# An opening loop that ends in another order, and modulation blocks moved from the heads to the branch projections

## The chip, the cores and the metric

The kernel runs on one core of a Trainium2 chip, as one launch. The metric is the device time of one execution in microseconds (us). The engines are TensorE (PE, matrix products), VectorE (DVE), ScalarE (ACT), GpSimd (POOL) and SyncE (SP, which here only issues DMAs). Each engine takes its instructions strictly in the order in which they stand; between engines semaphores order the work.

## The reference

Two layers of an encoder trunk on x of 256 tokens by 1024 channels, in f32. Each layer has two sub-layers, both modulated by a vector c:

```
mod = silu(c) @ ada_w[l] + ada_b[l]              # 6 x 1024: sh1, sc1, g1, sh2, sc2, g2
h = rmsnorm(x, norm_mix_w) * (1 + sc1) + sh1
x = x + g1 * mixer(h)
h = rmsnorm(x, norm_ffn_w) * (1 + sc2) + sh2
x = x + g2 * ((gelu(a) * val) @ w_down)          # a, val: halves of causal_conv3(h @ w_up)
```

The mixer projects h to 4784 columns. Columns c_q and c_kv go through an RMS norm and a second projection (w_uq, w_ukv) to the queries, keys and values of an attention with 8 heads; k_rope gets the rotary sine and cosine. The columns q_m and k_m go through a causal convolution of width 4 and a silu to the queries and keys of an mLSTM with 8 heads, whose gates i and f are 16 more columns. Both results are projected (w_br_mla, w_br_mlstm), merged by two sigmoid gates, and projected by w_out.

## The kernel before, in words

**Products.** Channels lie on the 128 partitions, tokens along the free axis. A weight tile of 128x1024 is loaded by SP (`raw`), rounded by ScalarE to a high part (`whi`, a CAST of about 1 us), and VectorE takes the rest (`wlo = raw - whi`). A product is three matmuls: whi with the high part of h (`hh`), whi with the low part (`hl`), wlo with `hh`. They follow each other on TensorE at about 0.117 us each for 256 tokens. A *unit* is 256 columns of w_in: 48 matmuls, two weight tiles. `W.take` (line 161) hands out a unit's weights, and the tiles of the next unit are split in the slots of this one (`emit_piece`).

**Evictions.** Each unit has a generator (`conv_silu`, `c_evict`, `misc_evict`, `gate_evict`, ...) that reads its PSUM bank. `unit` (line 265) runs slots of 12 matmuls; at the start of each slot `advance` takes every living generator one `yield` further. A scheduler in the framework then orders the instructions of an engine, but no further apart than a window (`act.window`, `dve.window`, line 172 on): window 0 keeps the written order.

**Opening** (lines 1222 to 1320). The six units in `FIRST` (line 68) of layer 0 are computed together, block k of 128 channels by block, while the modulation of that block is computed from its weights. The first `NATIVE` = 2 units of the list multiply in plain f32 (`ua` with `raw`), the other four in three matmuls. Units 0, 1 hold c_q and part of c_kv, unit 2 the rest of c_kv and the *misc* block (gates i, f and k_rope), unit 3 the first quarter of q_m, units 9 and 10 the output gate. At k = 7 `rotary_finish` (line 445) makes the sine and cosine, and a dummy tangent makes ScalarE load the table for tangent and exponential.

**Mixer of layer 0** (line 605). The evictions of the opening's units start (lines 963 on): c_evict (squares for the norm, and a copy `cqkv` scaled by the norm's weight), misc_evict, then conv_silu of unit 3. Units 4, 5, 6 follow, each with its convolution (6 `z` instructions on VectorE per unit, then a tangent and `qm`/`km`). Beside them run `c_norms` (statistics by matmuls with `shares`, a power on GpSimd, a broadcast by matmul, then `ua`, `ub` as the high and low part of the normed c) and `gates` (a transpose to `gs`, a chain of some 20 small instructions to `LF`, matmuls for sums over time to `CS`, a transpose to `ats`, a scan `M`, which is spread over partitions through DRAM to `tgl`). `DELAYS` and `LATER` say by how many slots each step is held back. Then come w_uq and w_ukv, ten *filler* units (v_m, output gate, merge gates) among which the 8 + 8 heads run, the branch projections (line 1090 on), w_out, and the feed-forward part.

**Heads.** An attention head makes scores (`bank<-kall,qall`), VectorE the maxima (`sm`), ScalarE the exponentials, VectorE the RECIPROCAL of the sum, ScalarE `w<-w,sm`, TensorE transposes (`bank<-cst,w`).

**Modulation blocks.** All other columns of mod are made by `pump` (line 344), one block of 128 outputs at a time: SP loads 128x1024 weights (`ada`, 512 KB, two buffers), and one VectorE instruction multiplies and sums. 24 blocks per layer have to be done by the end of the branch projections: in layer 0 and 1 they are pumped from the fillers (`fill`, line 1051), two per filler, three in the fillers of `FILLERS_3`.

Almost all instructions bear the line of the helper that records them (L184, or L186 for its other branch), so rows are told apart by tile names.

Of the kernel before, what the change touches and what calls it, by code (L numbers as in the profile page):

```python
# [60 lines left out]
FILLERS_3 = (4, 5, 6, 7)  # L61
# [6 lines left out]
FIRST = (0, 1, 2, 9, 10, 3)  # L68
NATIVE = 2
DELAYS = dict(kr=6, c=1, gates=3)  # L70
MLA_DELAY = (3, 2)
MASK_SLOTS = (4, 3) + (2,) * 6
LATER = (2, 2, 2, 1)
# [119 lines left out]
def hybrid_trunk(ctx, tc, a):  # L193
# [82 lines left out]
    def fm_steps(out, w, h, ks, msl, h0=0, start=True, stop=True):  # L276

        wh, wl = w
        hh, hl = h
        for i, k in enumerate(ks):  # L280
            first = start and i == 0
            last = stop and i == len(ks) - 1
            pe.matmul(out, wh.at(k, msl), hh[:, h0 + k, :], start=first, stop=False)
            pe.matmul(out, wh.at(k, msl), hl[:, h0 + k, :], start=False, stop=False)
            pe.matmul(out, wl.at(k, msl), hh[:, h0 + k, :], start=False, stop=last)
# [13 lines left out]
    def pair_slots(w, h, outs=None, split=False):  # L299


        if outs:
            def slot(ks):
                def run():
                    for k in ks:
                        for j in range(2):
                            fm_steps(outs[j], w, h, [k], slice(j * P, (j + 1) * P),
                                     start=k == 0, stop=k == KB - 1)
                return run

            return [slot(range(2 * i, 2 * i + 2)) for i in range(4)], outs
        if split:
            outs = [bank()[:, :T], bank()[:, :T]]
        else:
            b = bank()
            outs = [b[:, :T], b[:, T:2 * T]]

        def slot(j, k0):
            def run():
                fm_steps(outs[j], w, h, range(k0, k0 + 4), slice(j * P, (j + 1) * P),  # L320
                         start=k0 == 0, stop=k0 == 4)
            return run

        return [slot(j, k0) for j in range(2) for k0 in (0, 4)], outs
# [120 lines left out]
    def rotary_finish():  # L445
# [8 lines left out]
        act.activation(trigq[64:128], trig[64:128], AF.Copy, scale=qscale)  # L454
# [150 lines left out]
    def mixer(l, n, begun):  # L605
# [35 lines left out]
        def c_evict(i0, srcs):  # L641
            sqs = []
            for i, src in enumerate(srcs):
                sq = w256()
                act.activation(sq, src, AF.Square)
                b = i0 + i
                act.activation(cc_[:, b, :], src, AF.Copy, scale=ppc(l, "qn", b) if b < 3 else ppc(l, "kvn", b - 3))
                sqs.append(sq)
            yield
# [7 lines left out]
        def misc_evict(misc):  # L657
            act.activation(gt, misc[0:40], AF.Identity, bias=ppc(l, "gb", 0, 0, 40))
            r1 = w256()
            r2 = w256()  # L660
            dve.tensor_tensor(r1[64:96], misc[64:96], trig[64:96], ALU.mult)
            dve.tensor_tensor(r2[64:96], misc[96:128], trig[96:128], ALU.mult)
            kr = w256(tag="kr", bufs=1)
# [297 lines left out]


        if begun:
            h, first = begun
            for i in range(2):
                spawn(c_evict(2 * i, first[i][:2]))
            spawn(c_evict(4, first[2][:1]))
            spawn(misc_evict(first[2][1]))
            advance()
# [12 lines left out]
        for i in range(4):  # L982
            if 3 + i in first:
                spawn(conv_silu(2 * i, first[3 + i][:2]))
            else:
                slots, outs = pair_slots(W.take(), h)
# [64 lines left out]
        def fill():  # L1051
            i = left.pop(0)
            run_filler(i, ada=(0, 1, 2) if i in FILLERS_3 else (0, 2))
# [35 lines left out]

        ya = [(yah[:, 2 * i:2 * i + 2, :], yal[:, 2 * i:2 * i + 2, :]) for i in range(2)]  # L1090
        for c in range(2):
            for y, merge in ((ya, merge_a), (yl, merge_b)):
                w = W.take()
                for q in range(2):
# [10 lines left out]
                    unit([slot(0), slot(1)], merge(4 * c + 2 * q, b))  # L1105
# [145 lines left out]
    act.activation(warm, warm, AF.Sin)  # L1251
# [25 lines left out]
    for k in range(KB):  # L1277
# [23 lines left out]
        if k == KB - 1:  # L1301
            rotary_finish()
            act.activation(warm, warm, AF.Tanh)
# [14 lines left out]
    W.queue_split(W.at)  # L1318
    W.flush()
    pe.window, act.window, dve.window, gp.window = 1000, 8, 8, 2  # L1320
# [151 lines left out]
```

## Time and profile before

| what | value |
|---|---|
| three runs | 830.99, 831.08, 834.4 us; median 831.08 |
| the profiled execution | 829.05 us, of which the span from first to last instruction is 827.3 us |
| TensorE busy | 794.7 us of the span, 6452 matmuls |
| VectorE busy | 688.4 us |
| ScalarE busy | 502.0 us |
| mean granted TensorE clock | 0.986 of 2.4 GHz |
| DMA | 188.34 MB, 228 GB/s over the span |

Busy time counts an engine's instructions, and TensorE's are pipelined, so that short waits hide in it; a stretch is read by when its matmuls start and by what the engines beside it wait for. The clock that TensorE is granted is either full (2.4 GHz, shown as 1.00) or half (0.50). A wait is named with the engine that ended it.

### The profile page before, as it was taken

The numbers are of one execution on the slowest core, as the hardware profiler recorded it, in microseconds if no ns is written. First come the engines' busy times: TensorE is split into PE (matmuls) and PEld (weight loads), VectorE is DVE, ScalarE is ACT, GpSimd is POOL, SyncE is SP. The second block draws the span as 40 slices with busy tenths as digits, with TensorE's granted clock in tenths as the row PEclk, the third lists the DMA queues.
The fourth block names the chain that finished last, engine by engine and source line by source line (L and its number), as shares of the span: only waits on it lengthen the run. The fifth ranks groups of instructions, "written<-read, shape, count | busy, mean of one in ns | idle before, by whom it ended". The sixth has DMA issues, their size and how long they took to land.

```text
span 827.3 us, 16719 instructions
## 1 busy us (share of the span) xinstructions
PE 794.7 (96%) x6452; PEld 777.5 (94%) x6452; DVE 688.4 (83%) x1241; ACT 502.0 (61%) x918; POOL 79.0 (10%) x98
## 2 busy tenths in 40 slices
PE   5998989999999999999999999899999999999995
PEld 4998888999999999999999999799999999999995
DVE  5957988888989998888968987898887998888752
ACT  5674747664558766653548674676455876665551
POOL 4700020100010000000111001110011000000010
PEclk9998999999999999999999999999999999999998
DMA  9984587787765775468985468878754566546841
GB/s 338 396 287 133 184 328 259 237 284 258 239 219 175 244 239 182 142 199 305 327 328 179 133 203 303 278 250 284 255 180 159 178 204 197 182 142 202 296 125 51
DMA packets 57072, 188.34 MB, mean 228 GB/s; under 512 B 6576, under 2 KB 8352, under 8 KB 56992
## 3 DMA queue, kind: packets, MB, share of 16 engines
q1 hardware_dynamic: 55520, 183.89, 66.4%
q10 hardware_dynamic: 864, 2.23, 0.8%
q0 software_dynamic: 608, 1.16, 0.6%
q8 instruction: 50, 0.82, 0.4%
q14 instruction: 30, 0.25, 0.1%
HBM read 185.07 MB, written 1.06 MB: 225 GB/s over the span
## 4 chain that ended last, share of the span: by engine, by line
PE 57%; DVE 8%; DMA 4%; issue 3%; ACT 1%; DVEq 0%; POOLq 0%; POOL 0%; ACTq 0%
PE bank L184 57%; DMA ada<-in_ada 4%; DVE wlo L184 3%; DVE ada L184 2%; DVE w L184 1%; DVE hl L184 1%; DVE ub L184 0%; DVE z L184 0%; ACT whi L184 0%; DVE x L184 0%; ACT w L184 0%; DVE ua L184 0%; ACT ua L184 0%; ACT rs L184 0%; ACT sq L184 0%
## 5 line engine op out<-in xcount | busy, mean ns | idle before, releaser
L184 DVE TENSOR_TENSOR wlo<-raw,whi 128x1024 fp32r<-128x1024 f32 (+3 forms) x276 | 305.4, 1113 | 30.0 <-PE bank L184 10.5
L184 ACT CAST whi<-raw 128x1024 fp32r<-128x1024 f32 (+3 forms) x276 | 261.1, 955 | 114.1 <-PE bank L184 78.6
L184 PE MATMUL bank<-hh,whi 128*128 128x256 f32 x974 | 278.8, 287 | 0.0
L184 PE MATMUL bank<-hh,wlo 128*128 128x256 f32 x975 | 273.9, 281 | 1.1 <-DVE wlo L184 1.1
L184 PE MATMUL bank<-hl,whi 128*128 128x256 f32 x975 | 274.3, 282 | 0.0
L184 PEld LDWEIGHTS bank<-hh,wlo 128*128 128x128 f32 x975 | 184.3, 189 | 1.5 <-DVE wlo L184 1.5
L184 PEld LDWEIGHTS bank<-hl,whi 128*128 128x128 f32 x975 | 184.6, 189 | 0.9 <-DVE hl L184 0.3
L184 PEld LDWEIGHTS bank<-hh,whi 128*128 128x128 f32 x974 | 184.3, 189 | 1.1 <-issue 0.2
L184 DVE SCALAR_TENSOR_TENSOR ada<-ada,sact 128x1024 f32<-128x1024 f32 x96 | 118.4, 1237 | 21.0 <-DMA ada<-in_ada 20.7
L184 DVE SCALAR_TENSOR_TENSOR z<-bank,pp,z 128x255 f32<-128x255 f32 (+2 forms) x208 | 95.2, 477 | 17.0 <-ACT z L184 14.7
L184 PE MATMUL bank<-gh,wlo 128*128 128x256 f32 x352 | 99.0, 281 | 1.1 <-DVE wlo L184 1.1
L184 PE MATMUL bank<-gl,whi 128*128 128x256 f32 x352 | 99.1, 281 | 0.0
L184 PE MATMUL bank<-gh,whi 128*128 128x256 f32 x352 | 98.9, 281 | 0.0
L184 PEld LDWEIGHTS bank<-gh,wlo 128*128 128x128 f32 x352 | 66.3, 188 | 1.3 <-DVE wlo L184 1.3
L184 PEld LDWEIGHTS bank<-gl,whi 128*128 128x128 f32 x352 | 66.3, 188 | 0.0
L184 PEld LDWEIGHTS bank<-gh,whi 128*128 128x128 f32 x352 | 66.3, 188 | 0.0
L184 PE MATMUL bank<-ub,whi 128*128 128x256 f32 (+1 forms) x256 | 59.2, 282 | 0.0
L184 ACT ACTIVATE z<-bank,pp 128x256 f32<-128x256 f32 x96 | 49.1, 558 | 9.6 <-PE bank L186 5.6
L184 ACT ACTIVATE w<-z 128x256 f32<-128x256 f32 x60 | 25.0, 416 | 38.8 <-DVE z L184 37.1
L186 PE MATMUL bank<-hh,whi 128*128 128x256 f32 x146 | 46.1, 316 | 0.0
L184 PEld LDWEIGHTS bank<-ub,whi 128*128 128x128 f32 x256 | 43.9, 189 | 0.0
L186 PE MATMUL bank<-hh,wlo 128*128 128x256 f32 x145 | 42.7, 294 | 0.0
(253 smaller groups left out, 1390.3 us busy)
## 6 DMA issues: line engine op xcount, KB each, us to landing
ada<-in_ada SPq DMA_DIRECT2D x96, 512.0 KB, 5.1
raw<-in_w_up SPq DMA_DIRECT2D x88, 512.0 KB, 4.5
raw<-in_w_in SPq DMA_DIRECT2D x64, 512.0 KB, 5.6
raw<-in_w_down SPq DMA_DIRECT2D x32, 384.0 KB, 4.4
raw<-in_w_down SPq DMA_DIRECT2D x32, 320.0 KB, 3.9
raw<-in_w_out SPq DMA_DIRECT2D x16, 512.0 KB, 5.2
raw<-in_w_first SPq DMA_DIRECT2D x8, 512.0 KB, 8.1
raw<-in_w_bra SPq DMA_DIRECT2D x8, 512.0 KB, 5.2
```

The lines of the kernel that those rows point to most:

```text
L184: r = f(*args, **kw)
L186: r = f(*args, **kw)
```

## The change

Six things are written differently. (1) `FIRST` becomes 3, 2, 0, 1, 9, 10, so that unit 3 (a convolution's) and unit 2 (with the misc block) are the native ones and end first in each k. (2) The dummy activation ahead of the opening is a Silu and not a Sin, the dummy Tanh behind it is gone, and a dummy Exp comes later, in `widen`; `trigq` is moved behind the evictions. (3) ScalarE and VectorE stay in written order (window 0) from the opening until `widen` has been advanced twice: the convolution's first two steps, the gates' copy, the weight split, the rest of misc_evict, then c_evict. (4) c_evict takes the squares of its blocks first; in layer 0 the copies `cqkv` are made by VectorE. (5) The unit after the opening runs its matmuls with wlo behind those with whi (`late_lo`); the delays of the norm's sums, c_norms and gates change. (6) `FILLERS_3` is gone: every filler pumps two blocks, and every second of the eight half units of the branch projections pumps one, in both layers.

```diff
-FILLERS_3 = (4, 5, 6, 7)
+BRANCH_PUMPS = (0, 2, 4, 6)
-FIRST = (0, 1, 2, 9, 10, 3)
+FIRST = (3, 2, 0, 1, 9, 10)
-DELAYS = dict(kr=6, c=1, gates=3)
+DELAYS = dict(kr=6, shares=2, c=3, gates=1)
-LATER = (2, 2, 2, 1)
+LATER = (2, 2, 2, 0)
...
-            pe.matmul(out, wl.at(k, msl), hh[:, h0 + k, :], start=False, stop=last)
+            if not late_lo:
+                pe.matmul(out, wl.at(k, msl), hh[:, h0 + k, :], start=False, stop=last)
+        for i, k in enumerate(ks):
+            if late_lo:
+                pe.matmul(out, wl.at(k, msl), hh[:, h0 + k, :], start=False, stop=stop and i == len(ks) - 1)
...
-        act.activation(trigq[64:128], trig[64:128], AF.Copy, scale=qscale)
...
+                sqs.append(sq)
+            for i, src in enumerate(srcs):
                 b = i0 + i
-                act.activation(cc_[:, b, :], src, AF.Copy, scale=ppc(l, "qn", b) if b < 3 else ppc(l, "kvn", b - 3))
-                sqs.append(sq)
-            yield
+                gain = ppc(l, "qn", b) if b < 3 else ppc(l, "kvn", b - 3)
+                if begun:
+                    dve.tensor_scalar(cc_[:, b, :], src, gain, None, ALU.mult)
+                else:
+                    act.activation(cc_[:, b, :], src, AF.Copy, scale=gain)
+            for _ in range(1 + (DELAYS["shares"] if begun else 0)):
+                yield
...
+        def widen():
+
+            yield
+            yield
+            act.window = dve.window = 8
+            act.activation(warm, warm, AF.Exp)
...
-            for i in range(2):
-                spawn(c_evict(2 * i, first[i][:2]))
-            spawn(c_evict(4, first[2][:1]))
-            spawn(misc_evict(first[2][1]))
-            advance()
+            conv, misc = conv_silu(0, first[3][:2]), misc_evict(first[2][1])
+            cs = [c_evict(i0, src) for i0, src in ((4, first[2][:1]), (0, first[0][:2]), (2, first[1][:2]))]
+            W.queue_split(W.at)
+            next(conv)
+            next(conv)
+            next(misc)
+            W.flush()
+            next(misc)
+            for c in cs:
+                next(c)
+            act.activation(trigq[64:128], trig[64:128], AF.Copy, scale=qscale)
+            sides.extend([conv, misc] + cs[1:] + cs[:1] + [widen()])
...
-            run_filler(i, ada=(0, 1, 2) if i in FILLERS_3 else (0, 2))
+            run_filler(i, ada=(0, 2))
...
-                    unit([slot(0), slot(1)], merge(4 * c + 2 * q, b))
+                    unit([slot(0), slot(1)], merge(4 * c + 2 * q, b), ada=(0,) if half in BRANCH_PUMPS else ())
+                    half += 1
...
-    act.activation(warm, warm, AF.Sin)
+    act.activation(warm, warm, AF.Silu)
...
-            act.activation(warm, warm, AF.Tanh)
...
-    W.queue_split(W.at)
-    W.flush()
-    pe.window, act.window, dve.window, gp.window = 1000, 8, 8, 2
+    pe.window, gp.window = 1000, 2
```

Three places show what this does to the order.

The first is ScalarE at the end of the opening, from the second half of the rotary table on; `bank_211` is the first unit of `FIRST`, `bank_212` the second, `bank_213` to `bank_216` the four others, `whi_639` and `whi_680` the first weight tile of unit 4. Before:

```order
L184 ACTIVATE trig<-w_89_599 32x256
L184 ACTIVATE w_119_679<-bank_211 128x256
L184 ACTIVATE trigq<-trig 64x256
L184 ACT_TABLE_LOAD
L184 ACTIVATE warm<-warm 128x1
L184 CAST whi_639<-raw_635 128x1024
L184 CAST whi_643<-raw_637 128x1024
L184 ACTIVATE cqkv_676<-bank_211,pp 128x256
L184 ACTIVATE w_120_682<-bank_211 128x256
```

And now:

```order
L184 ACTIVATE trig<-w_89_599 32x256
L184 ACTIVATE z_669<-bank_211,pp 128x256
L184 ACTIVATE z_671<-bank_211,pp 128x256
L184 ACTIVATE gt_659<-bank_212,pp 40x256
L184 CAST whi_680<-raw_665 128x1024
L184 CAST whi_684<-raw_667 128x1024
L184 ACTIVATE w_123_692<-bank_212 128x256
L184 ACTIVATE w_124_695<-bank_213 128x256
L184 ACTIVATE w_125_697<-bank_213 128x256
L184 ACTIVATE w_126_701<-bank_214 128x256
L184 ACTIVATE w_127_703<-bank_214 128x256
L184 ACTIVATE trigq<-trig 64x256
```

The convolution's start (`z`), the gates' copy and the weight split (`whi`) now stand ahead of the squares (`w_123` on); the table load and the dummy behind it, which stood ahead of the split, stand six rows further down than what is shown, and the scaled copies `cqkv` are gone from ScalarE.

On VectorE at the same place, from the end of the rotary arguments (`w_89`), before; `z_721` is the convolution of unit 3, `gs` the transposed gates:

```order
L184 TENSOR_SCALAR w_89_599<-kr_105,csts 32x256
L184 TENSOR_TENSOR wlo_640<-raw_635,whi_639 128x1024
L184 TENSOR_TENSOR wlo_644<-raw_637,whi_643 128x1024
L184 TENSOR_TENSOR w_124_695<-bank_213,trig 32x256
L184 TENSOR_TENSOR w_125_696<-bank_213,trig 32x256
L184 TENSOR_TENSOR kr_699<-w_124_695,w_125_696 32x256
L184 SCALAR_TENSOR_TENSOR z_721<-bank_216,pp,z_721 128x255
L184 TENSOR_SCALAR sm_748<-bank_678 128x4
L184 SCALAR_TENSOR_TENSOR z_721<-bank_216,pp,z_721 128x254
L184 COPY gs_660<-bank_786 128x80
```

And now, with the same convolution as `z_669` and `z_671`, and `sm_790` the norm's sums:

```order
L184 TENSOR_SCALAR w_89_599<-kr_105,csts 32x256
L184 SCALAR_TENSOR_TENSOR z_669<-bank_211,pp,z_669 128x255
L184 SCALAR_TENSOR_TENSOR z_669<-bank_211,pp,z_669 128x254
L184 SCALAR_TENSOR_TENSOR z_669<-bank_211,pp,z_669 128x253
L184 SCALAR_TENSOR_TENSOR z_671<-bank_211,pp,z_671 128x255
L184 SCALAR_TENSOR_TENSOR z_671<-bank_211,pp,z_671 128x254
L184 SCALAR_TENSOR_TENSOR z_671<-bank_211,pp,z_671 128x253
L184 TENSOR_TENSOR wlo_681<-raw_665,whi_680 128x1024
L184 TENSOR_TENSOR wlo_685<-raw_667,whi_684 128x1024
L184 TENSOR_TENSOR w_121_688<-bank_212,trig 32x256
L184 TENSOR_TENSOR w_122_689<-bank_212,trig 32x256
L184 TENSOR_SCALAR cqkv_662<-bank_212,pp 128x256
```

All six `z` instructions of unit 3 stand ahead of the first weight split (`wlo`), where four of them stood behind the gates; behind them five copies `cqkv` are added, then `kr`, `gs` and the norm's sums.

The second place is the first attention head of layer 0 on VectorE, from the maxima (TENSOR_REDUCE) to the reciprocal and on; `wlo_1418` is half of a later filler's weights, `ada` a modulation block. Before:

```order
L184 TENSOR_REDUCE sm_1377<-bank_1352 128x1 x2
L184 TENSOR_TENSOR vaug_659<-bank_1291,ealo_657 128x4x64 x2
L184 SCALAR_TENSOR_TENSOR ada_1396,mod_84<-ada_1396,sact 128x1024
L184 TENSOR_TENSOR wlo_1418<-raw_1289,whi_1417 128x1024
L184 SCALAR_TENSOR_TENSOR ada_1421,mod_84<-ada_1421,sact 128x1024
L184 RECIPROCAL sm_1439<-sm_1414 128x2
L184 SCALAR_TENSOR_TENSOR w_263_1477<-bank_1386,w_258_1446 128x384
L184 MEMSET bank_1443 64x2x64
```

And now, with the same names:

```order
L184 TENSOR_REDUCE sm_1377<-bank_1352 128x1 x2
L184 TENSOR_TENSOR vaug_645<-bank_1291,ealo_643 128x4x64 x2
L184 SCALAR_TENSOR_TENSOR ada_1396,mod_84<-ada_1396,sact 128x1024
L184 TENSOR_TENSOR wlo_1418<-raw_1289,whi_1417 128x1024
L184 RECIPROCAL sm_1436<-sm_1414 128x2
L184 SCALAR_TENSOR_TENSOR ada_1447,mod_84<-ada_1447,sact 128x1024
L184 SCALAR_TENSOR_TENSOR w_262_1474<-bank_1386,w_257_1443 128x384
L184 MEMSET bank_1440 64x2x64
```

One modulation block less stands between the maxima and the RECIPROCAL. Layer 1 has the same two orders at this place.

The third is SP's queue at the end of the branch projections of layer 0 (`in_w_brl`, then `in_w_out`), before:

```order
L110 DMA raw_2354<-in_w_brl 128x1024
L339 DMA ada_2260<-in_ada 128x1024
L110 DMA raw_2356<-in_w_brl 128x1024
L339 DMA ada_2608<-in_ada 128x1024
L110 DMA raw_2422<-in_w_out 128x1024
L339 DMA ada_2647<-in_ada 128x1024
L110 DMA raw_2424<-in_w_out 128x1024
L110 DMA raw_2490<-in_w_out 128x1024
```

And now, the same stretch:

```order
L110 DMA raw_2346<-in_w_brl 128x1024
L343 DMA ada_2287<-in_ada 128x1024
L110 DMA raw_2415<-in_w_out 128x1024
L343 DMA ada_2354<-in_ada 128x1024
L110 DMA raw_2417<-in_w_out 128x1024
L343 DMA ada_2428<-in_ada 128x1024
L110 DMA raw_2486<-in_w_out 128x1024
L110 DMA raw_2488<-in_w_out 128x1024
L343 DMA ada_2496<-in_ada 128x1024
L110 DMA raw_2565<-in_w_out 128x1024
```

Loads of blocks now alternate with the tiles of w_out, where those tiles followed each other without a break from the second on.

## Rows read from the trace of the kernel before

**Rows 1.** The page, parts 1 and 2: busy time of engines; clock in 40 slices.

```profile
PE 794.7 (96%) x6452; PEld 777.5 (94%) x6452; DVE 688.4 (83%) x1241; ACT 502.0 (61%) x918; POOL 79.0 (10%) x98
PEclk9998999999999999999999999999999999999998
```

**Rows 2.** Windows: stretch, us, busy (count) of PE, PEld, DVE, ACT, POOL; clock, DMA.

```profile
55.49:103.86 48.37, 43.89 (x311) 41.53 (x311) 40.29 (x90) 31.71 (x58) 2.76 (x4) 0.89 0.55 174
59.69:66.52 6.83, 6.83 (x32) 6.53 (x32) 2.49 (x8) 3.70 (x6) 2.22 (x3) 0.50 0.76 216
80.17:83.58 3.41, 3.41 (x18) 3.41 (x18) 3.41 (x8) 1.44 (x2) 0.00 (x0) 0.50 0.48 147
124.54:127.96 3.42, 3.33 (x13) 2.94 (x14) 1.77 (x5) 2.64 (x8) 0.00 (x0) 0.50 0.88 308
177.50:200.00 22.50, 22.50 (x193) 22.50 (x192) 19.48 (x27) 10.18 (x13) 0.00 (x0) 1.00 0.87 304
520.49:523.90 3.41, 3.34 (x14) 3.08 (x14) 3.36 (x7) 2.34 (x7) 0.00 (x0) 0.50 0.82 238
```

**Rows 3.** Timeline, ScalarE, end of the opening: start, us, instruction, [idle before it].

```profile
52.19 0.38 ACT L184 ACTIVATE w<-bank 128x256 f32<-128x256 f32 x1 [1.56 <-PE bank L184]
53.02 1.28 ACT L184 ACT_TABLE_LOAD   x1
59.51 1.03 ACT L184 ACTIVATE z<-bank,pp 128x256 f32<-128x256 f32 x2
```

**Rows 4.** Timeline, VectorE, from there to the first block of modulation weights.

```profile
55.49 2.36 DVE L184 TENSOR_TENSOR wlo<-raw,whi 128x1024 fp32r<-128x1024 f32 x2 [5.45 <-ACT whi L184]
61.01 0.48 DVE L184 SCALAR_TENSOR_TENSOR z<-bank,pp,z 128x255 f32<-128x255 f32 x1
79.36 0.17 DVE L184 TENSOR_TENSOR LF<-g,LF 128x16 f32<-128x16 f32 x1
103.86 1.22 DVE L184 SCALAR_TENSOR_TENSOR ada<-ada,sact 128x1024 f32<-128x1024 f32 x1
```

**Rows 5.** Waits of VectorE, 52 to 104 us: in total, times, longest.

```profile
DVE gs L184 <- PE bank L186: 4.1, 1, 4.1
DVE w L184 <- ACT gt L184: 1.8, 1, 1.8
```

**Rows 6.** Timeline, TensorE: last native products; the gates' sums.

```profile
51.13 1.89 PE L184 MATMUL bank<-ua,raw 128*128 128x256 f32 x8
79.62 0.37 PE L186 MATMUL bank<-LF,cst 128*128 128x16 f32 x2 [2.87 <-issue]
```

**Rows 7.** Timeline, first heads of layer 0: VectorE, then TensorE.

```profile
120.61 1.78 DVE L184 TENSOR_TENSOR wlo<-raw,whi 128x1024 fp32r<-128x1024 f32 x1
122.32 1.74 DVE L184 SCALAR_TENSOR_TENSOR ada<-ada,sact 128x1024 f32<-128x1024 f32 x1
123.99 0.15 DVE L184 RECIPROCAL sm<-sm 128x2 f32<-128x2 f32 x1
...
124.63 1.09 PE L186 MATMUL bank<-cst,w 128*128 128x128 f32 x3 [2.73 <-ACT w L184]
```

**Rows 8.** Timeline, first heads of layer 1: VectorE, then TensorE.

```profile
516.10 1.21 DVE L184 TENSOR_TENSOR wlo<-raw,whi 128x1024 fp32r<-128x1024 f32 x1
518.39 1.28 DVE L184 SCALAR_TENSOR_TENSOR ada<-ada,sact 128x1024 f32<-128x1024 f32 x1 [1.08 <-DMA ada<-in_ada]
519.60 0.15 DVE L184 RECIPROCAL sm<-sm 128x2 f32<-128x2 f32 x1
...
520.24 1.09 PE L184 MATMUL bank<-cst,w 128*128 128x128 f32 x3 [2.70 <-ACT w L184]
```

**Rows 9.** Timeline, third head of layer 0: VectorE, then TensorE.

```profile
136.73 1.23 DVE L184 SCALAR_TENSOR_TENSOR ada<-ada,sact 128x1024 f32<-128x1024 f32 x1 [1.43 <-DMA ada<-in_ada]
137.88 0.55 DVE L184 SCALAR_TENSOR_TENSOR w<-bank,w 128x384 f32<-128x384 f32 x1
...
138.49 0.38 PE L186 MATMUL bank<-kall,qall 128*128 128x128 f32 x1 [1.35 <-DVE w L184]
```

More of the change, by code (lines that the diff above doesn't have):

```diff
@@ L273, in unit, with fm_steps @@
             spawn(evict)
-    def fm_steps(out, w, h, ks, msl, h0=0, start=True, stop=True):
+    def fm_steps(out, w, h, ks, msl, h0=0, start=True, stop=True, late_lo=False):
         wh, wl = w
@@ L297, in tm_steps, with pair_slots @@
             pe.matmul(out, hh[:, k, tsl], wl.at(k, csl), start=False, stop=last)
-    def pair_slots(w, h, outs=None, split=False):
+    def pair_slots(w, h, outs=None, split=False, late_lo=False):
         if outs:
@@ L320, in run @@
                 fm_steps(outs[j], w, h, range(k0, k0 + 4), slice(j * P, (j + 1) * P),
-                         start=k0 == 0, stop=k0 == 4)
+                         start=k0 == 0, stop=k0 == 4, late_lo=late_lo)
             return run
@@ L658, in misc_evict @@
             act.activation(gt, misc[0:40], AF.Identity, bias=ppc(l, "gb", 0, 0, 40))
+            if begun:
+                yield
             r1 = w256()
@@ L960, in mlstm_out @@
                                          ylh[:, b, :].bitcast(F32), ALU.mult, ALU.subtract)
+        def widen():
+            yield
+            yield
+            act.window = dve.window = 8
+            act.activation(warm, warm, AF.Exp)
         if begun:
             h, first = begun
-            for i in range(2):
-                spawn(c_evict(2 * i, first[i][:2]))
-            spawn(c_evict(4, first[2][:1]))
-            spawn(misc_evict(first[2][1]))
-            advance()
+            conv, misc = conv_silu(0, first[3][:2]), misc_evict(first[2][1])
[10 more added lines that the diff above has]
+            sides.extend([conv, misc] + cs[1:] + cs[:1] + [widen()])
         else:
@@ L982, in mixer @@
         for i in range(4):
[L983 to L986, printed above, removed]
+            if 3 + i not in first:
+                slots, outs = pair_slots(W.take(), h, late_lo=bool(first) and i == 1)
                 unit(slots, conv_silu(2 * i, outs))
@@ L1088, in merge_b @@
             dve.tensor_tensor(ml[:, m0:m0 + 2, :], v2(t), mh[:, m0:m0 + 2, :].bitcast(F32), ALU.subtract)
+        half = 0
         ya = [(yah[:, 2 * i:2 * i + 2, :], yal[:, 2 * i:2 * i + 2, :]) for i in range(2)]
```

## The prediction

> **What bounds the kernel now.** I read the page first: TensorE is busy 794.7 of 827.3 us [rows 1], so time can come only from waits of TensorE and from its clock. The clock is full but for the fourth slice [rows 1]. The windows [rows 2] show where: four stretches at half clock, 6.83 us from 59.69, 3.41 from 80.17, 3.42 from 124.54 and, in layer 1, 3.41 from 520.49. What runs at half clock takes twice as long, so they cost half of 17.1 us, 8.5 us. Three of the four lie in layer 0 between the end of the opening and the first heads. There the timelines show waits of TensorE as well: 2.87 us for the gates' sums at 79.62 [rows 6], 2.73 us at 124.63 [rows 7], 1.35 us at 138.49 [rows 9]; in layer 1 2.70 us at 520.24 [rows 8]. The waits are put down to issue or ScalarE, but read one row further back: the last write of `LF` ends at 79.36 + 0.17 = 79.53 [rows 4], and the transposes of the heads wait for ScalarE, which waits for the RECIPROCAL on VectorE [rows 7, 8]. So VectorE sets the pace in both places, by its queue.
>
> How far VectorE could be ahead: from 55.49 to 103.86, where the first modulation block starts [rows 4], it works 40.29 of 48.37 us [rows 2], idle 8.1. Two waits make 5.9 of these: 4.1 us for the gates' transpose and 1.8 us for ScalarE's copy of the gates [rows 5]. Ahead of 55.49 it waited another 5.45 us for the weight split [rows 4].
>
> **The change, part by part.** All sums are made against the profiled execution, 829.05 us; the median of the runs, 831.08, lies 2.03 above it, and I add that at the end.
>
> *Opening.* The opening's loop holds the same matmuls in another order and ends at the same time. VectorE's start: the first unit of FIRST is whole when ScalarE first reads its bank, at 52.19 [rows 3]. Now that is the convolution, whose two `z` took 1.03 us, 0.52 each [rows 3]; VectorE's six `z` can start at 52.7 and not behind the split at 55.49. They are work that it did later anyway, so they add nothing. Added are five `cqkv`; no such row is there. The nearest row, a z of as many columns that reads a bank too, is 0.48 us [rows 4], five of them 2.4; some of each lies beside its neighbour. I take 0.4 apiece, 2.0 us in all, and 1.5 to 2.4 as ends. The idle time: the two waits named go, since the gates' copy and the split now stand ahead of the squares on ScalarE, and since the z fill the rest; the other 2.2 us I leave in. A new wait is the norm's sums: `sm` now waits for five pairs of `shares` matmuls, which stand behind some 30 matmuls of unit 4, and behind it wait the split of unit 5 and the gates' chain. A walk down the two queues: VectorE has six z by 52.7 + 6 x 0.48 = 55.6 and the split of unit 4 (2.36 for its two halves [rows 4]) by 57.9, and with the rotary products, the five `cqkv` and small ones, some 3.7 together, is there at about 61.6. TensorE needs some 6.7 us from 55.6 for those matmuls at full clock, the gates' transposes and the pairs: 62.3. The difference is 0.7, 0.9 us with the way there and back. So the first block starts at 52.7 + 40.3 + 2.0 + 2.2 + 0.9 = 98.1, 5.8 us earlier. Does TensorE keep up? Its stretch of 43.89 busy us [rows 2] less 5.1 for its two half clocks is 38.8 us, to 94.3. It then waits some 3.8 us for VectorE, at the first tiles of w_uq and of w_ukv, whose splits stand behind the convolutions' z. I take **5.5 us** gained. Ends: 3.5, if 2 us more of idle time come in, and 7.5, if none does.
>
> *The table.* The number of table loads stays at six by the order. The one at 53.02 took 1.28 us [rows 3] ahead of the split; now it stands behind the split of unit 5, where ScalarE is done with it at about 64.4 and VectorE needs the exponential at 65.7. It costs nothing by the row, and 1.3 us are its cover. The Trainium skill (ScalarE: Activation LUTs, What ACT_TABLE_LOAD costs) adds about 1.38 us of drain to a load of 1.28 us. The row of the load agrees with its figure, but no drain stands in the trace between the neighbours; by the page the cover would be gone and 0.1 us lost.
>
> *Heads.* In layer 0 the modulation block at 122.32, 1.67 us to the reciprocal at 123.99 [rows 7], goes from ahead of the reciprocal to behind it. That wait of 2.73 falls to about 1.5 (the rest is the maxima's way, which now has a split more ahead): **1.2 us**. In layer 1 the same block had VectorE wait 1.08 us for its DMA and took 1.21 more [rows 8]. Without it the reciprocal stands behind the split that ends at 517.3, ScalarE is free at 518.0, and the transposes start near 518.45, not 520.24: **1.8 us**. At 138.49 VectorE had waited 1.43 us for a block's weights [rows 9], the eighth from the fillers; by then six are needed, so I take **1.1 us**; ends 0 and 1.35. If the waits shrink, the two half-clock stretches behind them go too: 1.7 us each, which I give 0.7: **2.4 us**.
>
> *Branch projections.* Four blocks per layer come here: each an `ada` of 1.22 [rows 4], 1.14 from start to start, and a load of 512 KB in SP's queue among those of w_out. VectorE is idle 22.50 - 19.48 = 3.0 us there [rows 2], so 1.6 of the 4.6 us are left over in layer 0, hidden behind the splits' lead of a unit. I charge **0.5 us**; ends 0 and 6, each of four blocks waiting 1.4 us for its weights as at 136.73 [rows 9].
>
> *New half clocks.* The waits at w_uq and w_ukv may bring a half-clock stretch: 1.7 us, of which part hides behind VectorE. I charge **1.2 us**; ends 0 and 5.1.
>
> Sum: 5.5 + 1.2 + 1.8 + 1.1 + 2.4 - 0.5 - 1.2 = 10.3 us. 831.1 - 10.3 = **820.8 us** (818.8 against the profiled execution).
>
> **The rivals.**
> First, the half clock follows the waits wherever they go. For it: each of the waits of 2.7 us or more here is followed by one [rows 2, 6, 7, 8]; against: the 1.35 us at 138.49 is not [rows 9]. Three waits are left in my walk (w_uq 2 us, w_ukv 3 us, the first head 1.5 us), 3 x 1.7 = 5.1 us in place of 1.2, and 824.7. The Trainium skill (TensorE: Matmul & The Clock Gate, HAM oscillation — how this bites in real kernels) has it that a wait between bursts of matmuls sends the array back to half rate, each time anew. By that rule the time is this 824.7; the trace agrees for the long waits.
>
> Second, VectorE does not use its early start: ScalarE, in written order, holds the second tangent behind the first `shares` matmuls, whose buffer it takes over, and the splits behind that. If 5 us of idle time stay, the opening brings 0.5 and the whole 5.0: 825.8. Against it: the tangent would be late by some 2 us and the split of unit 5 is needed only at 63.4.
>
> Third, the lead is lost at the heads: blocks and `tgl` come by DMA, and VectorE waits for them however early it is. Then layer 1 alone gains, 2 us: 829. Against it: their loads are issued when the block before is consumed, so they move along.
>
> Fourth, slower: the blocks in the branch projections stand in VectorE's queue ahead of the splits of w_out, and their loads in SP's queue between w_out's. It decides once each of the eight blocks waits 1.4 us as at 136.73 [rows 9], 2.6 us each, 21 us; less 2 x 3.0 idle [rows 2] 15 us are left against 10.8 gained, so about +4: 835. For it speaks the busy DMA there, 0.87 [rows 2]; against it that the same loads are taken out of a stretch as busy (0.88).
>
> That the change does not do what it says is excluded by the order, as far as that reaches.
>
> **How the numbers follow.** Forecast 0.58, first rival 0.15, second 0.13, third 0.08, fourth 0.06. About 0.5%, 4.2 us, is what a measurement of this kernel can tell from no change: faster is below 826.9. The forecast gives 0.56 of its chance to that, the first rival 0.13, the second 0.09, the third 0.02: 0.80. Slower takes 0.05 from the fourth; 0.15 is left for no change. From the ends of the terms the forecast reaches from 815.5 up; above, the range goes to 828.5, beyond the first two rivals, with the third and the fourth outside.
>
> **What would show it.** VectorE starts a z on the opening's first bank near 52.7 us; no half clock near 60; the gates' sums start near 74 without a wait; the first block starts near 98; the first head's transposes start near 118 instead of 124.63; layer 1's wait at 520.24 is near 1 us. Wrong would be: a first block later than 101 us, half clocks of more than 10 us in sum up to the heads, or new waits of TensorE between w_brl and w_up.

## The result, and the profile after

The changed kernel takes 820.25 us (median of four, 819.62 to 821.49) where the kernel before, on the same chip, takes 831.04: a ratio of 0.9893, interval 0.9862 to 0.9924. The medians alone differ by 10.8 us; the recorded ratio makes 8.9 us of 831. Forecast were 820.8 us and a gain of 10.3. The profiled execution took 819.74 us, its span is 818.0, 9.3 shorter than before. The page's busy times and its row of TensorE's clock answer to [rows 1]:

```profile
PE 788.9 (96%) x6452; PEld 773.1 (95%) x6452; DVE 690.8 (84%) x1246; ACT 499.2 (61%) x913; POOL 80.5 (10%) x98
PEclk7999999999999999999999999999999999999997
```

TensorE has the same 6452 matmuls and is busy 5.8 us less, which is mostly clock: from 22 us on and through the heads of layer 1 the stretches at half clock sum to 6.8 us and not 17.1, which is worth 5.1. The span fell by 3.5 us more than TensorE's busy time, which is waits. The 7 with which the row of the clock begins is no loss against before. There the trace has no record of the clock ahead of 22.14 us, and the profile shows 1.00 for want of one; but the first eight native products took 3.78 us in both kernels, in the changed one under a recorded 0.50, and the last eight of the kernel before 1.89 [rows 6]. For the same reason the mean clocks of two executions can be compared only if both have, or both lack, such a record. The windows of the stretches at half clock, with a short one at full clock ahead of them, and of VectorE from its first `z` to the first modulation block, answer to [rows 2] (columns as there):

```profile
7.50:10.92 3.42, 1.05 (x8) 0.97 (x8) 3.28 (x8) 2.48 (x4) 0.00 (x0) 1.00 1.03 411
10.92:21.16 10.24, 6.86 (x22) 5.85 (x23) 7.96 (x14) 6.01 (x14) 9.14 (x15) 0.50 1.03 407
62.12:65.53 3.41, 3.41 (x17) 3.41 (x18) 3.07 (x6) 3.33 (x6) 3.02 (x3) 0.50 0.90 282
92.84:96.25 3.41, 3.41 (x17) 3.16 (x17) 3.35 (x5) 1.17 (x2) 0.54 (x1) 0.50 0.67 221
52.40:100.17 47.77, 43.09 (x321) 41.33 (x320) 43.01 (x95) 31.32 (x56) 3.79 (x4) 0.93 0.61 198
```

Both stretches behind the first heads, at 124.54 and at 520.49 before, are gone; between the opening and the heads there are two as before, one of them shorter. VectorE needs 47.77 us for that way, 43.01 of them work. Its timeline, at the places that answer to [rows 4] and to the heads of [rows 7]:

```profile
52.40 2.94 DVE L184 SCALAR_TENSOR_TENSOR z<-bank,pp,z 128x255 f32<-128x255 f32 x6 [3.34 <-ACT z L184]
...
58.95 2.21 DVE L184 TENSOR_SCALAR cqkv<-bank,pp 128x256 f32<-128x256 f32 x5 [0.45 <-ACT w L184]
...
99.03 1.23 DVE L184 TENSOR_TENSOR wlo<-raw,whi 128x1024 fp32r<-128x1024 f32 x1 [1.80 <-PE bank L186]
100.17 1.22 DVE L184 SCALAR_TENSOR_TENSOR ada<-ada,sact 128x1024 f32<-128x1024 f32 x1
...
105.41 0.76 DVE L184 TENSOR_TENSOR vaug<-bank,ealo 128x256 f32<-128x256 f32 x2 [1.73 <-PE bank L186]
109.55 1.22 DVE L184 SCALAR_TENSOR_TENSOR ada<-ada,sact 128x1024 f32<-128x1024 f32 x1 [2.25 <-DMA ada<-in_ada]
118.43 0.15 DVE L184 RECIPROCAL sm<-sm 128x2 f32<-128x2 f32 x1
```

VectorE starts early, as forecast, but at 99.03 it waits for TensorE. TensorE's timeline shows why. Its waits there, then its first head in layer 0 (now 119.55, 124.63 before) and the longest wait at a head that is left, in layer 1:

```profile
90.64 0.39 PE L186 MATMUL bank<-ua,wlo 128*128 128x256 f32 x1 [2.93 <-DVE wlo L184]
92.55 0.38 PE L186 MATMUL bank<-ua,wlo 128*128 128x256 f32 x1 [1.29 <-DVE wlo L184]
119.55 0.84 PE L186 MATMUL bank<-cst,w 128*128 128x128 f32 x3 [0.16 <-ACT w L184]
512.19 0.92 PE L184 MATMUL bank<-kall,qall 128*128 128x128 f32 x4 [1.03 <-DVE w L184]
```

TensorE waited 4.2 us for the splits of w_ukv, and then VectorE 1.8 us for TensorE: two queues that hold each other up.

Where the 9.3 us of the span went is read from TensorE's timeline at seven marks that all kernels share: the last native product, and in each layer the first matmul of the heads' first filler, the first of the branch projections with `ub` and `wlo`, and the first of w_down. Each entry is the length of a stage, us, and in the last columns what it differs from before: as forecast, as measured, and in the first two runs below, "opening alone" and "blocks alone".

| stage (TensorE) | before | after | forecast | measured | opening alone | blocks alone |
|---|---|---|---|---|---|---|
| start to the last native product | 52.64 | 51.79 | 0 | -0.85 | 0.00 | -1.39 |
| to the first filler of layer 0 | 49.40 | 47.74 | -4.3 | -1.66 | -1.40 | -2.67 |
| heads of layer 0 | 85.70 | 79.82 | -3.5 | -5.87 | -1.40 | -4.14 |
| branch projections to w_up | 174.28 | 175.13 | +0.25 | +0.85 | +0.04 | +0.32 |
| w_down to layer 1's first filler | 135.73 | 136.16 | 0 | +0.43 | -0.27 | -0.62 |
| heads of layer 1 | 83.99 | 80.84 | -3.0 | -3.15 | +0.44 | -3.79 |
| branch projections to w_up | 172.75 | 173.19 | +0.25 | +0.45 | +0.02 | +0.11 |
| w_down to the end | 72.79 | 73.29 | 0 | +0.50 | +0.23 | +0.50 |

(Forecast: 5.5 - 1.2 in the opening; 1.2 + 1.1 and half of the 2.4 of clock in layer 0's heads; 1.8 and the other half in layer 1's; 0.5 of loss shared by the layers.) The sum came out, but not stage by stage: the opening brought 2.6 us less than forecast, the heads of layer 0 2.4 more, and 0.85 came from ahead of the first mark.

The last two columns are one execution each, and not a typical one: the profiled execution of the opening alone is the slowest of its twelve (826.74 us, median 823.29), that of the blocks alone the fastest of its seven (817.37, median 822.61). They sum to -2.3 and -11.7 us. The blocks alone keep the old opening, and yet their second stage is 2.67 us shorter, with 3.41 us of half clock in it and not 10.24. A difference of that size in one stage can be the clock's alone; what each part is worth is read from the medians below.

### The profile page after: what moved, and what is told of

The parts are those of the page before. It is cut to its first block, busy times and chain, and to the rows that moved or that the text cites. A ratio compares the mean times of both kernels' runs of the same rounds, so it can differ in the third digit from the quotient of the medians.

```text
span 818.0 us, 16722 instructions
## 1 busy us (share of the span) xinstructions
PE 788.9 (96%) x6452; PEld 773.1 (95%) x6452; DVE 690.8 (84%) x1246; ACT 499.2 (61%) x913; POOL 80.5 (10%) x98
## 4 chain that ended last, share of the span: by engine, by line
PE 70%; DVE 13%; DMA 8%; issue 5%; ACT 3%; POOL 1%; POOLq 0%; DVEq 0%; ACTq 0%
PE bank L184 61%; PE bank L186 9%; DVE wlo L184 5%; DMA ada<-in_ada 4%; DVE ada L184 2%; DVE w L184 2%; DMA raw<-in_w_in 1%; DMA raw<-in_w_out 1%; DMA raw<-in_w_down 1%; ACT whi L184 1%; DVE z L184 1%; ACT w L184 1%; DVE hl L184 1%; DVE ua L184 1%; DMA raw<-in_w_up 1%
## 5 line engine op out<-in xcount | busy, mean ns | idle before, releaser
L184 PE MATMUL bank<-hh,wlo 128*128 128x256 f32 x975 | 273.6, 281 | 1.1 <-DVE wlo L184 1.1
L184 PE MATMUL bank<-hl,whi 128*128 128x256 f32 x975 | 274.1, 281 | 0.0
L186 PE MATMUL bank<-hl,whi 128*128 128x256 f32 x145 | 40.9, 285 | 0.0
```

Source lines behind the costliest of these rows:

```text
L184: r = f(*args, **kw)
L186: r = f(*args, **kw)
```

## The experiments

Each ran beside the kernel before; ratios are to it, with their intervals, since its median was 827.2, 828.2 and 829.0 us in the three sets of runs. Theory: VectorE's queue sets the pace, each part of the change makes room in it, and the parts add up. Rivals: the lead of the opening pays only with the thinned heads, or not at all, and the half clock decides.

**The opening alone** (the blocks put back):

```diff
-BRANCH_PUMPS = (0, 2, 4, 6)
+BRANCH_PUMPS = ()
+FILLERS_3 = (4, 5, 6, 7)
-            run_filler(i, ada=(0, 2))
+            run_filler(i, ada=(0, 1, 2) if i in FILLERS_3 else (0, 2))
```

> The changed kernel with the modulation blocks put back where they were before (three in each of the fillers 4 to 7, none in the branch projections): the new opening and nothing else. By the terms of the prediction the opening is worth 5.5 us less 1.2 for new half clocks, and the heads keep their waits and both half-clock stretches behind them: about 4.3 off 831.0, 826.7, with first heads' transposes waiting over 2 us in both layers. Rival: VectorE's lead is paid out at the first heads whatever stands among them, so that layer 0's share of the gain (8.4 us up to the branch projections by the two traces) comes with the opening alone and only layer 1 keeps its wait: about 823, with no half clock near 120 us. Second rival: the lead is worth nothing without the thinned heads: 829 or more.

**The blocks alone** (the kernel before with the same two places changed the other way):

> The kernel before with only the modulation blocks moved (two in every filler of the heads, four in the branch projections of each layer). By the terms of the prediction 1.2 + 1.8 + 1.1 + 2.4 - 0.5 = 6.0 us off 831.0: 825.0, with both half-clock stretches of the first heads gone. Rival: in layer 0 the heads gain from the opening's lead and not from the blocks; then layer 1's 3.2 us are left, less 1.7 us lost at the branch projections and w_out: about 829.5, with a wait over 2 us and a half clock near 124 us in layer 0.

Opening alone: 823.29 against 827.16, ratio 0.9956 (0.9941 to 0.9971), 3.9 us. Blocks alone: 822.61, ratio 0.9938 (0.9907 to 0.997), 4.5 us, single times from 817.4 to 827.1. Together 8.4 us of the 8.9 that the ratio of the change makes of 829: they add up, as far as intervals of 2.4 to 4.9 and 2.5 to 7.7 us can tell. Neither rival of the first run holds as a whole, nor does the rival of the second, which left 1.5 us and a wait over 2 us at layer 0's first head. The timeline of TensorE in the opening alone shows how the lead is paid out; first heads of layer 0, third head of layer 0, first heads of layer 1:

```profile
121.00 0.84 PE L187 MATMUL bank<-cst,w 128*128 128x128 f32 x3 [0.50 <-ACT w L185]
...
134.27 1.01 PE L187 MATMUL bank<-kall,qall 128*128 128x128 f32 x4 [1.99 <-DVE w L185]
...
516.52 0.84 PE L185 MATMUL bank<-cst,w 128*128 128x128 f32 x3 [2.01 <-ACT w L185]
```

The wait of 2.73 us at the first head falls to 0.50 without any block moved, where the expectation left over 2 us. But the third head's wait grows from 1.35 to 1.99, with a half-clock stretch of 3.41 us behind it at 134.98 where before had one at 124.54. The wait stands behind a block that waited for its load; VectorE's timeline there:

```profile
132.51 1.23 DVE L185 SCALAR_TENSOR_TENSOR ada<-ada,sact 128x1024 f32<-128x1024 f32 x1 [2.62 <-DMA ada<-in_ada]
```

So part of my third rival, the lead lost to the blocks' loads, is what happens where the heads are full; with the thinned heads no profile of the changed kernel has a wait over 1.02 us of TensorE at a head of layer 0. In the blocks alone the same first head waits 0.89:

```profile
119.19 0.84 PE L186 MATMUL bank<-cst,w 128*128 128x128 f32 x3 [0.89 <-ACT w L184]
```

**The last convolution evicted later**, to see whether TensorE and VectorE hold each other up at w_ukv:

```diff
-                unit(slots, conv_silu(2 * i, outs))
+                unit(slots, delayed(6 if first and i == 3 else 0, conv_silu(2 * i, outs)))
```

> The changed kernel with the eviction of the last convolution of layer 0 started six slots later, so that its six z and two km stand behind the splits of w_ukv in VectorE's queue. Theory: VectorE's queue holds TensorE back at w_ukv (2.93 + 1.29 us, and a half clock of 3.41 us behind them), and TensorE then holds VectorE back (1.80 us at 99.03, 1.73 at 105.41). Both waits shrink: w_ukv under 1 us, no half clock near 93, filler 0 starts by 96 instead of 99.53, and the time falls by about 3 us to 817. Rival: VectorE has the same work up to the first heads and is as late there; the time stays at 820. Second rival: the bank and the z that are held longer stop TensorE or ScalarE elsewhere: 822 or more.

> The kernel with the last convolution of layer 0 evicted six slots later (as in the run e3_conv_late), beside the changed kernel. In the traces filler 0 started 5.2 us earlier with it than in the changed kernel, the first head's transposes 3.1, the second norm 0.7. Theory: the lead is used up at the heads, by VectorE's waits for the loads of modulation blocks (2.69 us at 105.42), and at w_out; 0 to 1 us are left, 0.987 to 0.989 of the kernel before. Rival: the half clock that goes with the wait at w_ukv is worth 1.7 to 3.4 us on the average of the runs: 0.985 or less.

> The changed kernel once more, as the measure for the three beside it: 0.988 to 0.989 of the kernel before.

The first run gave 816.28, ratio 0.9877 (0.9855 to 0.99), too close to the change's 0.9893 of another chip to tell. Side by side: 816.44, ratio 0.9849 (0.9829 to 0.9868), against the changed kernel's 819.16, 0.9888 (0.9871 to 0.9904): 2.7 us. The stage ahead of the first filler falls from 47.77 us (the changed kernel in the same set) to 42.14, 5.6 us, and the theory's mechanism is there. TensorE's wait at w_ukv, then VectorE's wait for a block's load:

```profile
88.54 0.39 PE L186 MATMUL bank<-ua,wlo 128*128 128x256 f32 x1 [0.67 <-DVE wlo L184]
```

```profile
106.26 1.23 DVE L184 SCALAR_TENSOR_TENSOR ada<-ada,sact 128x1024 f32<-128x1024 f32 x1 [2.88 <-DMA ada<-in_ada]
```

No half clock follows near 93 us. Of the 5.6 us, 1.6 are lost in layer 0's heads, 2.0 between layer 0's w_down and layer 1's first filler, and 1.8 in layer 1's heads, where a half-clock stretch stands at 509.73 that only this profile has. Of the two expectations of the side-by-side run the theory's 0 to 1 us was too little; the ratio stands at the edge of the rival's 0.985 or less. Whether the missing half clock makes the difference, as that rival has it, is not shown by two profiles.

**One block fewer in the second filler of the heads**, one more in the branch projections, on top of the late convolution:

```diff
-            run_filler(i, ada=(0, 2))
+            run_filler(i, ada=(2,) if i == 1 else (0, 2))
-BRANCH_PUMPS = (0, 2, 4, 6)
+BRANCH_PUMPS = (0, 1, 2, 4, 6)
```

> The same with one modulation block less in the second filler of the heads of each layer (the block that waited 2.69 us for its load) and one more in the branch projections, at half unit 1. Theory: VectorE waits less for loads ahead of the first head, which keeps 1 to 2 us of its lead up to the branch projections; there the fifth block costs some 0.5 us per layer, since the four cost 1.7 in both: the time is within 1 us of the kernel it is made from, and the loss stands between the branch projections and the second norm. Rival: DMA is full in both places, the load waits at the next filler instead, and with the branch's loss the time is 1 us longer or more.

815.37, ratio 0.984 (0.9818 to 0.9863), 1.1 us below its parent where within 1 us was expected, and the fastest median of all, though not told apart from the parent. Layer 0's heads take 79.54 us in place of 81.96, and the stage of the branch projections 177.06 in place of 174.88: won in one place, lost in the other. VectorE's longest waits in the two places are both for loads, with a DMA share of 1.02 from 103 to 108 us and 0.87 from 174 to 179:

```profile
107.00 1.23 DVE L184 SCALAR_TENSOR_TENSOR ada<-ada,sact 128x1024 f32<-128x1024 f32 x1 [1.73 <-DMA ada<-in_ada]
...
178.30 1.23 DVE L184 SCALAR_TENSOR_TENSOR ada<-ada,sact 128x1024 f32<-128x1024 f32 x1 [2.32 <-DMA ada<-in_ada]
```

**The branch's blocks in pairs**, also on top of the late convolution: `BRANCH_PUMPS = (0, 1, 4, 5)`.

> The same as e10_conv_late_beside with the four blocks of the branch projections at half units 0, 1, 4 and 5, so that none stands between the last two halves and the merge that w_out waits for. Theory: the wait of TensorE at w_out for ScalarE's mh (0.9 us, 204.0) is VectorE's merge standing behind the block of half unit 6: it goes, and 0.5 to 1 us of the time with it. Rival: two blocks in a row wait for their loads (2.38 us at 182.57 with one between), the splits of w_out behind them are late, and the time is the same or 1 us longer.

819.63, ratio 0.9888 (0.9867 to 0.9909), 3.2 us more than its parent, with intervals that just touch. The theory fell: TensorE's wait for ScalarE's `mh` is still there with 1.1 us. So is the rival's wait, in VectorE's timeline:

```profile
182.42 1.23 DVE L184 SCALAR_TENSOR_TENSOR ada<-ada,sact 128x1024 f32<-128x1024 f32 x1 [3.03 <-DMA ada<-in_ada]
```

The branch stage is 1.7 us longer than the parent's; another 2.9 stand in layer 0's heads, with a half-clock stretch at 119.00 that the parent did not have there, so the size of the rival's effect is not settled by the total.

**Two of w_out's blocks moved to w_up** in the changed kernel: `OUT_PUMPS = ((3, 4, 5), ())`, `UP_PUMPS = ((4, 5, 6, 7, 8), ())`.

> The changed kernel with two of the five modulation blocks of layer 0's w_out moved into w_up (units 5 and 7). Theory: the 1.3 us that the changed kernel loses between the branch projections and the second norm of layer 0 are VectorE's, which with the four new blocks stands behind at w_out (TensorE's gaps of 1.07 and 1.13 us near 206 and 213); they go, and the time falls to about 819. Rival: w_up has no room either, and what is won at w_out is lost there: 820 to 821. Second rival: the loss has another cause (ScalarE's mh, the loads of w_out), and the gaps stay: 820.

819.17, ratio 0.9904 (0.9883 to 0.9924): no gain. TensorE's waits from 190 to 262 us (total, times, longest), with two blocks fewer in w_out:

```profile
PE bank L184 <- DVE wlo L184: 1.2, 2, 0.6
PE bank L184 <- ACT mh L184: 0.9, 1, 0.9
```

In the changed kernel they are 1.4 and 0.8. They stay, so these two blocks are not their cause, and the theory fell against its second rival; what makes ScalarE's `mh` late is left open.

**The parts of the opening**, undone one by one, with the changed kernel beside them:

> The changed kernel itself, beside the kernel before on this chip, as the measure for the runs of this call: a ratio of 0.989 as first measured. What is open is the half clock: in the profiles of the runs so far the stretch near 62 us is there in two kernels with this opening and missing in two others with the same opening. If it hangs on the instructions alone it is there again; if not, it may be missing or stand elsewhere, and the time moves by 1.7 us for each stretch of 3.41.

It gave 817.98, ratio 0.9878 (0.9851 to 0.9905).

```diff
-FIRST = (3, 2, 0, 1, 9, 10)
+FIRST = (0, 1, 2, 9, 10, 3)
```

> The changed kernel with the units of the opening's loop in the old order, so that the convolution, which ScalarE still evicts first, is complete last (about 54.8 us and not 51.3). Theory: VectorE's first z starts near 56 and not 52.40, 3.4 us later; the split of unit 4 and all behind it is later by as much, TensorE waits some 3 us for it near 56, the first modulation block starts near 103, and the time is 3 to 5 us above the changed kernel's (823.5 to 825 where the kernel before takes 831). Rival: VectorE's early start is not used, because it waits for TensorE behind w_ukv anyway (1.80 us at 99.03): under 1 us above the changed kernel.

824.67, ratio 0.9949 (0.9932 to 0.9967): 6.7 us lost, more than the 3 to 5 expected. VectorE's first `z`, and TensorE's waits for the splits of unit 4:

```profile
55.88 2.94 DVE L184 SCALAR_TENSOR_TENSOR z<-bank,pp,z 128x255 f32<-128x255 f32 x6 [6.28 <-ACT z L184]
```

```profile
57.19 0.39 PE L186 MATMUL bank<-hh,whi 128*128 128x256 f32 x1 [2.40 <-ACT whi L184]
60.01 1.22 PE L186 MATMUL bank<-hh,wlo 128*128 128x256 f32 x4 [1.28 <-DVE wlo L184]
```

The 3.7 us of waits stand where the theory put them, the first modulation block starts at 106.36 (near 103 expected), and with the waits comes more half clock: two stretches of 6.83 us and one of 3.41 up to the heads, against one of 6.83 in the changed kernel's profile of the same set. With the old order of units the new opening is not told apart from the blocks alone (0.9938): as far as these intervals tell, what it brings hangs on the convolution, which is evicted first, being complete first.

```diff
-    act.activation(warm, warm, AF.Silu)
+    act.activation(warm, warm, AF.Sin)
 ...
             rotary_finish()
+            act.activation(warm, warm, AF.Tanh)
```

> The changed kernel with the old loads of ScalarE's tables: the sine's table ahead of the opening, and the tangent's table loaded behind the rotary sines and not shared with them. Theory: the table of a load costs nothing on either side: it stands in the 1.69 us that ScalarE waits for the convolution's bank ahead of 51.34, of which it takes 1.28 + 0.2, z starts when it did, and the time is within 0.5 us of the changed kernel's. Rival: a load has a cost behind its row as well (by the Trainium skill, ScalarE: Activation LUTs, What ACT_TABLE_LOAD costs, a drain of about 1.38 us): z, and VectorE behind it, start some 1.2 us later, and the time is 1 us longer or more.

819.63, ratio 0.9908 (0.9873 to 0.9943): not told apart from the changed kernel by its time, but by ScalarE's timeline:

```profile
49.67 0.41 ACT L184 ACTIVATE trig<-w 32x256 f32<-32x256 f32 x1
50.10 1.28 ACT L184 ACT_TABLE_LOAD   x1
51.40 0.20 ACT L184 ACTIVATE warm<-warm 128x1 f32<-128x1 f32 x1
52.14 1.02 ACT L184 ACTIVATE z<-bank,pp 128x256 f32<-128x256 f32 x2 [0.54 <-PE bank L184]
```

With the load back, ScalarE still waits 0.54 us for the bank: one load fewer at this place is worth nothing that these runs show, and nothing is seen of a drain, since the load starts 0.02 us after the sine's end and the next instruction 0.02 after its own.

```diff
-                if begun:
-                    dve.tensor_scalar(cc_[:, b, :], src, gain, None, ALU.mult)
-                else:
-                    act.activation(cc_[:, b, :], src, AF.Copy, scale=gain)
+                act.activation(cc_[:, b, :], src, AF.Copy, scale=gain)
```

> The changed kernel with the five products cqkv back on ScalarE. Theory: VectorE gets back the 2.21 us that they take there, and TensorE's waits at w_ukv (2.93 and 1.29 us) shrink by about 2; but ScalarE's splits of unit 5 stand 2 us later behind them, and TensorE, which takes unit 5 at 62.28 as soon as they are there, waits there for as long: 0 to 2 us above the changed kernel. Rival: ScalarE has room (61% busy), the wait at unit 5 hides, and the time is 2 us or more below the changed kernel's.

821.85, ratio 0.9921 (0.9897 to 0.9945): 3.9 us more by the medians, beyond the upper end expected, with intervals that just overlap. TensorE waits 0.61 us for unit 5's split, not 2; but VectorE idles 3.96 us for the norm's sums and is then held at the first filler by a TensorE that is later:

```profile
64.11 0.16 DVE L184 TENSOR_SCALAR sm<-bank 128x4 f32<-128x4 f32 x1 [3.96 <-PE bank L186]
...
101.75 1.22 DVE L184 TENSOR_TENSOR wlo<-raw,whi 128x1024 fp32r<-128x1024 f32 x1 [3.02 <-PE bank L186]
```

In the three profiles of the changed kernel the first of these waits is 0.4 to 0.5 us, the second 1.80 to 2.25. By the medians the five products belong on VectorE: the 2.21 us that they cost it cover a wait that is longer without them.

## Why the prediction was right, and where it was not

*The opening, 5.5 us: too large, and the step that failed can be named.* VectorE starts at 52.40 (52.7 forecast), and the five `cqkv` take 2.21 us (2.0, ends 1.5 to 2.4). The first modulation block stands at 100.17, not 98.1, so 3.7 us earlier than before. The step was "It then waits some 3.8 us for VectorE, at the first tiles of w_uq and of w_ukv": TensorE does wait, 4.2 us and at w_ukv alone, and I took it as free, but for the 1.2 us charged to new half clocks, since VectorE would set the pace. But the half clock behind it slows TensorE, and VectorE then waits 1.80 us for it at 99.03 and 1.73 at 105.41; without the first it would have been there near 98.4. That the order of VectorE's queue at w_ukv is the cause is shown by the late convolution, which takes 5.6 us out of this stage. Measured at that block, net of the 1.2, the forecast was 4.3 us; the three profiles of the changed kernel have 3.7, 4.6 and 2.9, of which 0.85, 1.2 and 0.1 come from the program's start, so that 2.8 to 3.4 are left. In TensorE's stages the opening itself gave 1.66 us (2.21 and 1.63 in the two other profiles), which is no more than the half clock's: 6.83 us of stretches there in place of 10.24. The lead of VectorE is paid out at the first heads, where the opening alone brings 1.40 more.

*The heads of layer 0, 3.5 us: too small.* Blocks alone gave 4.14, both 5.87. The sum missed that an earlier VectorE also takes the rest of the wait at the first head: I left 1.5 us of it, and 0.16 is left.

*The heads of layer 1, 3.0: right*, 3.15 (2.81 and 3.82 in the two other profiles of the changed kernel), and nothing without the blocks (+0.44 in the opening alone). The first head's wait of 2.70 is gone, and one of 1.03 stands one head later.

*The branch projections, 0.5: right in kind.* The two stages lose 1.3, 0.3 and 1.4 us in the three profiles of the changed kernel and 0.4 in the blocks alone. The wait for a block's load that decides the fourth rival is there once:

```profile
182.57 1.23 DVE L184 SCALAR_TENSOR_TENSOR ada<-ada,sact 128x1024 f32<-128x1024 f32 x1 [2.38 <-DMA ada<-in_ada]
```

It is not there at each of eight blocks; and a fifth block (2.2 us in layer 0) or pairs (1.7) show that the four stand near what the stretch bears. Of the signs of being wrong, new waits of TensorE between w_brl and w_up, a small one came: for ScalarE's `mh`, 0.8, 0.2 and 0.4 us in layer 0 of the three profiles, and 0.6 and 0.9 in layer 1 of two of them; before has none.

*The half clock, 2.4 gained and 1.2 lost.* Both stretches at the heads went, as forecast. Of new ones the changed kernel has 3.41 us at w_ukv (1.7 of loss). "No half clock near 60" was wrong in this profile, and right in another of the same kernel (next section). My first rival is right for w_ukv: each profile with the wait of 2.9 us there has a half clock that begins in it or soon behind it. The Trainium skill (TensorE: Matmul & The Clock Gate, HAM oscillation — how this bites in real kernels) tells of waits of about 3 to 5 us between bursts of matmuls that each of them sends the clock back to half; the waits here are no longer than 2.9. The rival decided nothing in the end, because the first head's wait went almost whole.

*The table, 0: right*, by the timeline above; the drain that the Trainium skill (ScalarE: Activation LUTs, What ACT_TABLE_LOAD costs) adds is not seen.

*The second rival* (VectorE does not use its early start) failed: undoing the order of units loses 6.7 us. So the number came out through two errors of 2.5 us that cancel, opening against heads, which are two ends of one thing: where a lead of VectorE is cashed in. And 0.85 us came from the start of the program, where the change swaps nothing but the function of a dummy activation: two other profiles of the changed kernel have stage one at 51.45 and 52.56 us, before at 52.64. That the number came within 1 us is luck: against the one profile of before, the three of the changed kernel are 9.3, 13.3 and 9.4 us shorter.

Of the other signs, the gates' sums start at 76.04 without a wait (near 74 forecast), and the first head's transposes at 119.55 (near 118).

## What to carry to other kernels

When an engine's lead is the gain, follow it to the place where another engine first waits for it, and count both directions: a wait called free can make the waited-for engine wait in turn. Put what the other engine needs next (here the splits of w_ukv) ahead of work that is needed late (the last convolution), and only then look for places for filler work. Filler work can be moved from one busy place to another only as far as the second bears it: four blocks per layer moved out of the heads gained 4.5 us alone, and the fifth lost in the new place what it won in the old.

## What the runs showed that I had not expected

The half clock is not a function of the instructions alone. The first profile of the changed kernel has a stretch at half clock at 62.12 us (windows above), with no wait over 0.35 us in the 8 us ahead of it. Of the two other profiles of the same kernel one has it and one has not, in the columns of [rows 2]:

```profile
62.92:66.34 3.42, 3.42 (x17) 3.42 (x17) 3.13 (x6) 3.36 (x6) 3.03 (x3) 0.50 0.88 256
```

```profile
62.00:65.41 3.41, 3.41 (x30) 3.35 (x30) 3.35 (x7) 3.38 (x7) 1.79 (x3) 1.00 0.82 232
88.83:95.65 6.82, 5.45 (x23) 4.91 (x24) 6.70 (x10) 1.16 (x2) 0.54 (x1) 0.50 0.52 167
```

Behind the wait at w_ukv the stretch is 3.41 us long in two of the three and 6.82 in the third.

The traces of the experiments show what the stretch near 62 us goes with. Eleven profiles have the units of the opening in the new order. In seven of them the clock rose to full for the opening at 21.16 to 22.34 us, and each has a half-clock stretch that begins at 62.12 to 63.30, or at 66.00 in the one run (`cqkv` on ScalarE) that waits 0.61 us just ahead of it. In the other four it rose at 19.44 to 20.56, and none has one there. With the old opening it is alike: in the kernel before it rose at 22.14 and a stretch stands at 59.69, in the blocks alone it rose at 19.25 and none stands until 77.28. So this stretch goes with when the clock rose at the start, and that differs between executions of one kernel; why is not shown.

The eight one-column products with `ones` near 9.7 us took 1.87 us in one profile, as before, and 1.05 and 1.12 in the two others, in which the opening began some 0.8 us earlier: that is the gain of the first stage, which no instruction of the change explains. In these two a stretch of 3.41 us at full clock covers them, the one at 7.50 shown with the result and one at 6.91; the third has none on record, and neither has before. Over whole runs the clock makes a spread that no single profile shows: the blocks alone took 817.4 us at a mean clock of 0.993 and 827.1 at 0.980, though 0.006 of such a difference can be the missing record of the start.
